# Splitting the tokens beside the norm, sorting them in one run, and another order of the expert slots

## The chip, the core and the metric

One core of a Trainium2 chip runs the whole kernel in one launch. The metric is the device time in microseconds of that launch. All data are 32-bit floats in HBM; 32 experts of 12 MiB each lie there, of which only those that some token chose are read.

## The reference

A decoder layer on 256 tokens of 2048 features. Its first half mixes a dilated attention (1024 columns) with a gated linear recurrence (1024 columns), projects the two and normalises:

```python
x = _layer_norm(ALPHA * x + mix, ln1_g, ln1_b)
moe = _hier_moe(x.reshape(B * S, D), router_grp_w, ..., w1, w3, w2)
x = _layer_norm(ALPHA * x + moe, ln2_g, ln2_b)
```

`_hier_moe` takes the best of 4 groups for each token, then the best 2 of that group's 8 experts, and adds up the two experts' outputs with their weights. One expert is

```python
(jax.nn.silu(xblk @ w1[e]) * (xblk @ w3[e])) @ w2[e]      # w1, w3: 2048 x 512, w2: 512 x 2048
```

So 512 (token, expert) pairs are spread over up to 32 experts, unevenly: on these inputs 28 experts have tokens.

## The kernel before, in words

The first half of the layer (input projection, recurrence, attention, output projection, L73 to L473) ends at about 402 us and is not touched. What follows is:

**Norm (L476 to L487).** The statistics give `rstd` and `nmr`. ScalarE normalises `X` (128 partitions, 2 token tiles, 2048 columns) in place, in four instructions: 512 and then 1536 columns for each tile.

**Router (L488 to L611).** On DVE and TensorE, with small tiles: the logits, the best group, the best two experts, each pair's place in the order by expert (`place`), and the one-hot matrices `srt` (128 x 512, one for each token tile), which put every token into its two places. `ints` holds the counts and the slots' experts; L592 writes the count of experts in use, which every engine loads at L1013 before the slots begin. L597 and L603 are two small exponentials on ScalarE for the weights. The gains' and the residual's rows come over GpSimd's queue (L642, L644). Up to L641 or so the order on each engine is a planner's, by readiness; from `manual_schedule` in `experts` on it is that of the code.

**Slots (L1014 to L1035).** The experts run one after the other in 32 slots: experts 0 and 1 first, then by rank in size, in the order of `_R` (L37): slot 2 + k takes the expert of rank `_R[k]`, rank 0 being the largest. The order mixes large with small. A slot's code has arms by its count of tokens: 32 rows (`up32`, matmuls at L824), 64 rows (`up64`, L846), 128 (`up128`, L868) and twice 128. Slots 0, 1 and those of rank 0 to 6 choose among arms by the count; rank 7 to 14 always take 64 rows, and rank 15 on 32. With 28 experts in use, ranks 0 and 1 take 128 rows, ranks 2 to 14 take 64, the other 13 slots 32. A slot's matmuls of w1 and w3 come in four quarters, with two weight tiles each; then a transpose, the silu, the matmuls of w2 (L911), and the sums into `X` through matmuls with the one-hot `ohT` (L921, L926).

**Ring (L697 to L750).** The weights come in loads of 1 MiB, 12 for an expert, on SyncE's queue, in order, into a ring of 15 tiles. `advance` (L751) says how many tiles TensorE has given back; a load whose tile is free is issued, else the queue waits. After 15 loads a sixteenth tile (`spare`, slot18, which holds the split tokens and `srt` until slot 0 is over) joins in.

**Sort (L759 to L775), called by slot 0.** For each of 16 groups of 128 columns: ScalarE copies the group into `hi` in a rounded form (L766), DVE takes the rest `lo` (L767), four matmuls with `srt` (L770) put the tokens in order, DVE or ScalarE evicts with gain and offset (L773, L775). `hi` and `lo` have two buffers in `parts`. In slot 0, `before(q)` calls `sort` ahead of each quarter of the expert's own matmuls, and the tables of `by_slot` (L614, matmuls at L195 and L628) and the residual (L799, matmuls at L808) between them; each of the four arms has this code.

Of the kernel before, what the change touches and what calls it, by code (L numbers as in the profile page):

```python
# [9 lines left out]
FT = mybir.dt.float32  # L10
# [10 lines left out]
D = 2048  # L21
# [15 lines left out]
_R = [15, 0, 16, 1, 17, 2, 3, 18, 4, 5, 19, 6, 7, 20, 8, 9, 21, 10, 11, 22, 12, 13, 14] + list(range(23, 30))  # L37
# [42 lines left out]
def hybrid_layer(ctx, tc, x, w_in, conv_w, conv_b, lru_wa, lru_ba, lru_wx, lru_bx, lru_lambda,  # L80
# [403 lines left out]
    for c in (slice(0, 512), slice(512, D)):  # L484
        for t in range(2):
            a = X[:, t, c]
            nc.scalar.activation(a, a, AF.Identity, bias=nmr[:, t:t + 1], scale=rstd[:, t:t + 1])  # L487
    ar = slot(19, "ar19")  # L488
# [57 lines left out]
    parts = slot(18, "parts", FR)  # L546
# [101 lines left out]
    experts(ctx, tc, X, acc, ar, blk, parts, srt, by_slot, Rs, Gs, ints, gb, lnr, w1, w3, w2, ident, iota, slot, sm, misc, bank,  # L648
# [31 lines left out]
def experts(ctx, tc, x1, acc, f, blk, parts, srt, by_slot, Rs, Gs, ints, gb, lnr, w1, w3, w2, ident, iota, slot, sm, misc, bank,  # L680
# [4 lines left out]

    xs = [slot(i, f"xs{i}").rearrange("p (j s) -> p j s", j=4) for i in (8, 11, 9, 12)]

    xt = slot(6, "xt").rearrange("p (j c) -> p j c", j=16)
    hl = parts[:, 0:1024].rearrange("p (b h t m) -> p b h t m", b=2, h=2, t=2)
# [7 lines left out]
        "xp": Rot(bank[0:2]),  # L697
# [10 lines left out]
    xv = x1.rearrange("p t (q m j) -> p t q j m", q=4, j=4)  # L708
# [41 lines left out]
    def advance(n=0):  # L750

        done[0] += n
        while nxt[0] < len(order) and need[nxt[0]] <= done[0]:
            load(nxt[0])
            nxt[0] += 1
# [4 lines left out]
    def sort(q):  # L760

        for jj in range(4):
            j = 4 * q + jj
            hi, lo = (hl[:, j % 2, h] for h in range(2))
            src = xv[:, :, q, jj, :]
            nc.scalar.activation(hi, src, AF.Copy)  # L766
            nc.vector.tensor_tensor(out=lo, in0=src, in1=hi.bitcast(FT), op=OP.subtract)  # L767
            xp = R["xp"].tile()
            for k, (t, part) in enumerate(((0, hi), (1, hi), (0, lo), (1, lo))):
                nc.tensor.matmul(xp, lhsT=part[:, t, :], rhs=srt[t], start=k == 0, stop=k == 3)  # L770
            dst = xs[q][:, jj, :]
            if jj % 2:
# [184 lines left out]
    side = [None]  # L957

    def expert(i):

        def before(q):
            if i == 0:
                for k in ((0, 1), (2,), (3,), ())[q]:
                    sort(k)
                    fetch(0, 0, quarters=(k,))
                if q in (1, 2):
                    next(side[0])
                if q == 3:
                    residual(0, 1)

        def small(up, n):
            if i == 0:
                side[0] = by_slot()
            else:
                ahead(i + 1)
            gt, ohT = up(i, before)
            if i == 0:
                ahead(1)
                residual(2, 3)
            dn(i, gt, ohT, n)  # L980

        def first():
            if i == 0:
                list(by_slot())
                for q in range(4):
                    sort(q)
                residual(0, 1, 2, 3)

        def wide():
            first()  # L990
            gt, ohT = up128(i, 0, True)
            ahead(i + 1)
            dn(i, gt, ohT, 128)

        def huge():
            first()
            done[0] += 8
            halves = [up128(i, c, False) for c in (0, 128)]
            ahead(i + 1)
            for c, (gt, ohT) in enumerate(halves):  # L1000
                dn(i, gt, ohT, 128, c == 1)
        arms = [(32, lambda: small(up32, 32)), (64, lambda: small(up64, 64)), (128, wide), (256, huge)]
        if i < 2:
            choose(count(81 + i), arms)
        elif bound(i) > 64:
            choose(count(32 + i), arms[1:])
        else:
            evs.clear()
            arms[bound(i) > 32][1]()
            evs.clear()  # L1010

    advance()
    n_all = nc.values_load(ints[0:1, 80:81], min_val=2, max_val=32, skip_runtime_bounds_check_because=WHY)  # L1013
    for i in range(TAIL):  # L1014
        if i < 2:
            expert(i)
            if not i:
                spare = slot(18, "ring18")
                homes[:] = [spare if t is None else t for t in homes]
            continue  # L1020
# [54 lines left out]
```

## Time and profile before

| | us |
|---|---|
| median of 3 runs | 1373.0 (1368.92 to 1380.15) |
| the profiled execution | 1368.74 |
| its span, first to last instruction | 1366.9 |
| TensorE busy | 1192.3 (87%) |
| DVE, ScalarE, GpSimd busy | 493.9, 308.3, 71.0 |
| bytes moved by DMA | 419.80 MB |

Busy shares are averages over stages with different limits: the first half of the layer (to 402 us) has TensorE as its limit, and the slots have to be read by themselves, by what the weights' queue and TensorE wait for.

### The profile page before, as it was taken

What the parts mean: (1) busy time and instruction counts of PE and PEld (TensorE: products, weight loads), DVE (VectorE), ACT (ScalarE), POOL (GpSimd) and SP (SyncE); (2) the same over time, 40 slices, a digit from 0 to 9 for tenths busy, and PEclk for the clock granted to TensorE, in tenths of its full rate; (3) what the DMA queues carried; (4) which work ended last, traced back from release to release, by engine and by line L of the source; (5) the groups of instructions that cost most, each with busy time, mean ns of one, the idle gap of its engine ahead of it and who ended that gap; (6) DMA issues with size and microseconds to landing.
All of it is one profiled execution on the core that took longest, in us unless ns stands there. A gap on an engine that the chain in (4) does not pass through costs nothing. (4 is left out here: it accounts for less than half of the span.)

```text
span 1366.9 us, 16357 instructions
## 1 busy us (share of the span) xinstructions
PE 1192.3 (87%) x6065; PEld 645.8 (47%) x6065; DVE 493.9 (36%) x776; ACT 308.3 (23%) x554; POOL 71.0 (5%) x75
## 2 busy tenths in 40 slices
PE   6989999999985777999987897788899897998875
PEld 6988899988872332333432222222333332332222
DVE  4678545457544342121121111121322212213336
ACT  4366444434332211011110100110201101100001
POOL 5111102130000000000000000000000000000001
PEclk9999999999995778999999989999999898999775
DMA  9634653464840469979889999899999999999992
GB/s 317 197 138 140 203 182 131 130 247 155 316 146 1 149 231 420 417 306 421 306 344 402 371 421 365 334 421 401 418 420 420 418 420 420 419 420 420 419 382 96
DMA packets 81721, 419.80 MB, mean 307 GB/s; under 512 B 7008, under 2 KB 7344, under 8 KB 38448
## 3 DMA queue, kind: packets, MB, share of 16 engines
q1 hardware_dynamic: 80384, 416.31, 77.0%
q0 software_dynamic: 912, 1.31, 0.5%
q8 instruction: 70, 1.15, 0.3%
q10 hardware_dynamic: 288, 0.48, 0.1%
q14 instruction: 67, 0.55, 0.1%
HBM read 432.75 MB, written 2.10 MB: 318 GB/s over the span
## 5 line engine op out<-in xcount | busy, mean ns | idle before, releaser
L926 DVE TENSOR_TENSOR xres<-bank,xres 128x512 f32<-128x512 f32 x224 | 145.7, 685 | 243.8 <-PE bank L921 243.2
L846 PE MATMUL bank<-ring,xt 128*64 128x512 f32 x792 | 203.4, 655 | 16.6 <-issue 16.6
L921 PE MATMUL bank<-sm,ar 32*128 32x512 f32 (+2 forms) x448 | 174.6, 742 | 20.0 <-DVE xres L926 10.0
L911 PE MATMUL bank<-ring,sm 128*32 128x512 f32 (+2 forms) x840 | 163.6, 625 | 32.0 <-DVE sm L858 12.1
L165 DVE TENSOR_TENSOR wl<-raw,wh 128x2048 fp32r<-128x2048 f32 (+1 forms) x59 | 129.6, 2202 | 106.3 <-ACT wh L164 106.3
L195 PE MATMUL bank<-xh,wl 128*128 128x256 f32 x512 | 148.2, 291 | 6.2 <-DVE wl L165 6.2
L195 PE MATMUL bank<-xh,wh 128*128 128x256 f32 x512 | 148.9, 291 | 1.2 <-ACT wh L164 1.2
L195 PE MATMUL bank<-xl,wh 128*128 128x256 f32 x512 | 148.4, 290 | 0.0
L824 PE MATMUL bank<-ring,xt 128*32 128x512 f32 x768 | 115.3, 690 | 31.2 <-issue 25.7
L164 ACT ACTIVATE wh<-raw 128x2048 fp32r<-128x2048 f32 (+1 forms) x59 | 107.6, 1826 | 146.7 <-PE bank L195 128.5
L846 PEld LDWEIGHTS bank<-ring,xt 128*64 128x64 f32 x792 | 64.5, 151 | 146.9 <-issue 146.8
L899 DVE COPY ar<-bank 128x256 f32<-128x256 f32 x28 | 11.9, 424 | 317.6 <-PE bank L898 317.6
L921 PEld LDWEIGHTS bank<-sm,ar 32*128 32x128 f32 (+2 forms) x448 | 64.4, 209 | 123.4 <-DVE xres L926 69.7
L911 PEld LDWEIGHTS bank<-ring,sm 128*32 128x32 f32 (+2 forms) x840 | 48.3, 130 | 124.5 <-issue 76.6
L195 PEld LDWEIGHTS bank<-xh,wl 128*128 128x128 f32 x512 | 101.0, 198 | 7.1 <-DVE wl L165 6.8
L195 PEld LDWEIGHTS bank<-xh,wh 128*128 128x128 f32 x512 | 101.3, 198 | 1.8 <-ACT wh L164 1.6
L195 PEld LDWEIGHTS bank<-xl,wh 128*128 128x128 f32 x512 | 101.3, 198 | 0.4
L824 PEld LDWEIGHTS bank<-ring,xt 128*32 128x32 f32 x768 | 28.8, 123 | 102.8 <-issue 95.3
L917 ACT ACTIVATE sm<-bank 128x512 f32<-128x512 f32 x47 | 28.1, 597 | 201.8 <-PE bank L911 193.8
L851 ACT ACTIVATE sm<-bank 128x512 f32<-128x512 f32 x13 | 7.8, 597 | 273.7 <-PE bank L846 273.7
L868 PE MATMUL bank<-ring,xt 128*128 128x512 f32 x120 | 57.8, 641 | 0.0
L674 POOL TENSOR_TENSOR xres<-xres,offset 128x512 f32<-128x512 f32 x4 | 6.4, 1611 | 940.5 <-ACT xres L673 940.5
(274 smaller groups left out, 1170.3 us busy)
## 6 DMA issues: line engine op xcount, KB each, us to landing
ring<-in_w_dram SPq DMA_DIRECT2D x330, 1024.0 KB
raw<-in_w_in_dram SPq DMA_DIRECT2D x39, 1024.0 KB
misc<-in_w_dram SPq DMA_DIRECT2D x22, 1024.0 KB
raw<-in_w_out_dram SPq DMA_DIRECT2D x16, 1024.0 KB
xres<-in_x_dram SPq DMA_DIRECT2D x4, 512.0 KB
out_dram<-xres SPq DMA_DIRECT2D x8, 256.0 KB
raw<-in_w_in_dram SPq DMA_DIRECT2D x4, 256.0 KB
offset<-in_ln_b_dram SPq DMA_DIRECT2D x1, 1024.0 KB
```

The source lines that it names most:

```text
L164: nc.scalar.activation(h[:, e], r[:, e], AF.Copy)
L165: nc.vector.tensor_tensor(out=l[:, e], in0=r[:, e], in1=h[:, e].bitcast(FT), op=OP.subtract)
L195: nc.tensor.matmul(o, lhsT=l, rhs=r, start=start, stop=stop, skip_group_check=True)
L824: nc.tensor.matmul(hp[p0:p0 + 32, :], lhsT=xt[:, j + par, i % 2 * 64:i % 2 * 64 + 32], rhs=wp(i, nm, j + par), start=j == 0, stop=j == 14)
L846: nc.tensor.matmul(hp[c * 64:c * 64 + 64, :], lhsT=xt[:, j, i % 2 * 64:i % 2 * 64 + 64], rhs=wp(i, nm, j), start=j == 0, stop=j == 15)
L851: nc.scalar.activation(hs, hp, AF.Copy)
L868: nc.tensor.matmul(hp[k], lhsT=xt[:, j, :], rhs=wp(i, nm, j), start=j == 0, stop=j == 15)
L899: nc.vector.tensor_copy(ohT, tr[:, 0:2, :])
L911: nc.tensor.matmul(yp[n * h:n * h + n, :], lhsT=gt[:, j, 0:n], rhs=w[:, c:c + 512], start=j == 0, stop=j == 3)
L917: nc.scalar.activation(y, yp, AF.Copy)
L921: nc.tensor.matmul(cp, lhsT=ohT[n * h:n * h + n, t, :], rhs=y[n * h:n * h + n, :], start=True, stop=True)
L926: nc.vector.tensor_tensor(out=a, in0=cp, in1=a, op=OP.add)
```

## The change

The normalisation goes by quarters of 512 columns, and behind each quarter its two blocks of 256 columns (4 blocks of 128 x 2 tiles wide) are split: ScalarE copies `hi`, GpSimd subtracts `lo`, one instruction for each token tile. Seven blocks of 1024 have room (`parts`, and slots 9, 12 and 6, which get their old use after the sort); the eighth is split into the first one's place when that is sorted. The sort runs in one piece ahead of slot 0 for every arm, on four PSUM banks, with the two steps of `by_slot` after blocks 2 and 4. Then come the gather for slots 0 and 1, the sixteenth ring tile, and the slots. `early` loads the two counts of slots 0 and 1 ahead of that of the experts.

```diff
-_R = [15, 0, 16, 1, 17, 2, 3, 18, 4, 5, 19, 6, 7, 20, 8, 9, 21, 10, 11, 22, 12, 13, 14] + list(range(23, 30))
+_R = [15, 16, 17, 0, 18, 19, 1, 20, 2, 3, 4, 21, 5, 6, 7, 8, 22, 9, 10, 11, 12, 13, 14] + list(range(23, 30))
...
-    for c in (slice(0, 512), slice(512, D)):
+    parts = slot(18, "parts", FR)
+    stage = [parts[:, 0:1024]]
+    for i in (9, 12, 6):
+        b = slot(i, f"stage{i}", FR)
+        stage += [b[:, 0:1024], b[:, 1024:2048]]
+    stage.append(stage[0])
+    xv = X.rearrange("p t (q m j) -> p t q j m", q=4, j=4)
+
+    def split(b):
+        hi, lo = (stage[b][:, 512 * h:512 * h + 512].rearrange("p (t j m) -> p t j m", t=2, j=2) for h in range(2))
+        src = xv[:, :, b // 2, b % 2 * 2:b % 2 * 2 + 2, :]
         for t in range(2):
-            a = X[:, t, c]
+            nc.scalar.activation(hi[:, t], src[:, t], AF.Copy)
+        for t in range(2):
+            nc.gpsimd.tensor_tensor(out=lo[:, t], in0=src[:, t], in1=hi[:, t].bitcast(FT), op=OP.subtract)
+        return hi, lo
+    jobs = []
+    for q in range(4):
+        for t in range(2):
+            a = X[:, t, q * 512:q * 512 + 512]
             nc.scalar.activation(a, a, AF.Identity, bias=nmr[:, t:t + 1], scale=rstd[:, t:t + 1])
+        for b in (2 * q, 2 * q + 1):
+            if b < 7:
+                jobs.append(split(b))
...
-        "xp": Rot(bank[0:2]),
+        "xp": Rot(bank[0:4]),
...
-    homes = list(ring)
+    homes = ring + [None]
     need = [0] * len(homes)
     for k in range(len(order)):
         homes.append(homes[k])
         need.append(k + 1)
-        if k == 13:
-
-            homes.append(None)
-            need.append(k + 2)
...
-    def sort(q):
-
-        for jj in range(4):
-            j = 4 * q + jj
-            hi, lo = (hl[:, j % 2, h] for h in range(2))
-            src = xv[:, :, q, jj, :]
-            nc.scalar.activation(hi, src, AF.Copy)
-            nc.vector.tensor_tensor(out=lo, in0=src, in1=hi.bitcast(FT), op=OP.subtract)
-            xp = R["xp"].tile()
+    def sort(b):
+
+        q = b // 2
+        hi, lo = jobs[b]
+        xps = [R["xp"].tile() for _ in range(2)]
+        for jj, xp in enumerate(xps):
             for k, (t, part) in enumerate(((0, hi), (1, hi), (0, lo), (1, lo))):
-                nc.tensor.matmul(xp, lhsT=part[:, t, :], rhs=srt[t], start=k == 0, stop=k == 3)
+                nc.tensor.matmul(xp, lhsT=part[:, t, jj, :], rhs=srt[t], start=k == 0, stop=k == 3)
+        if b == 0:
+            jobs.append(split(7))
...
         def before(q):
-            if i == 0:
-                for k in ((0, 1), (2,), (3,), ())[q]:
-                    sort(k)
-                    fetch(0, 0, quarters=(k,))
-                if q in (1, 2):
-                    next(side[0])
-                if q == 3:
-                    residual(0, 1)
+            if i == 0 and q == 3:
+                residual(0, 1)
...
     advance()
+    early = [count(81 + i) for i in range(2)]
     n_all = nc.values_load(ints[0:1, 80:81], min_val=2, max_val=32, skip_runtime_bounds_check_because=WHY)
+    xs = []
+    side = by_slot()
+    for b in range(8):
+        sort(b)
+        if b in (2, 4):
+            next(side)
+
+    xt = slot(6, "xt").rearrange("p (j c) -> p j c", j=16)
+    fetch(0, 0)
+    ahead(1)
+    spare = slot(18, "ring18")
+    homes[:] = [spare if t is None else t for t in homes]
+    advance()
```

## Rows read from the trace of the kernel before

**Rows 1.** Windows: stretch, length, busy PE PEld DVE ACT POOL, PEclk, DMA share, GB/s.

```profile
404.00:440.00 36.00, 17.50 (x57) 10.88 (x58) 16.71 (x75) 12.83 (x19) 1.63 (x3) 0.59 0.09 30
440.00:520.00 80.00, 61.98 (x332) 27.77 (x335) 28.23 (x51) 15.02 (x33) 0.00 (x0) 0.78 0.53 202
520.00:950.00 430.00, 368.12 (x1498) 134.98 (x1492) 86.32 (x156) 47.94 (x138) 0.00 (x0) 0.90 0.93 378
950.00:1330.00 380.00, 340.93 (x1608) 113.52 (x1608) 99.82 (x182) 43.55 (x129) 0.00 (x0) 0.91 1.01 419
```

**Rows 2.** Timeline of SyncE's queue: start us, us, the weights' loads issued.

```profile
403.47 0.33 SPq L748 DMA_DIRECT2D misc<-in_w_dram  x1
444.47 47.49 SPq L748 DMA_DIRECT2D ring<-in_w_dram  x9
...
1314.93 0.33 SPq L746 DMA_DIRECT2D ring<-in_w_dram  x1
```

**Rows 3.** Waits of SyncE's queue, 404 to 450: us, times, longest us.

```profile
SPq L748 <- PE bank L824: 28.0, 1, 28.0
```

**Rows 4.** Timeline of ScalarE: the norm, and the sort's first copy.

```profile
404.23 4.63 ACT L487 ACTIVATE xres<-xres,st 128x512 f32<-128x512 f32 x4 [0.36 <-DVE st L482]
...
416.60 0.65 ACT L766 ACTIVATE parts<-xres 128x256 fp32r<-128x256 f32 x1 [7.54 <-DVE ar L591]
```

**Rows 5.** Groups of instructions by line and shape, 416 to 475.

```profile
L770 PE MATMUL bank<-parts 128*128 128x512 f32 x64 | 25.9, 533 | 19.6 <-ACT parts L766 16.6 <-DVE parts L767 3.0
L766 ACT ACTIVATE parts<-xres 128x256 fp32r<-128x256 f32 x16 | 9.9, 646 | 7.5 <-DVE ar L591 7.5
...
L195 PE MATMUL bank<-ar,sm 32*128 32x32 f32 x8 | 1.9, 399 | 1.5 <-DVE sm L630 1.5
...
L628 PE MATMUL bank<-con,ar 128*32 128x128 f32 x4 | 1.0, 414 | 0.0
```

**Rows 6.** Timeline of TensorE: matmul spacing, slot 0's end, first matmuls of slots.

```profile
391.95 0.40 PE L195 MATMUL bank<-wh,al 128*128 128x512 f32 x1
392.18 0.39 PE L195 MATMUL bank<-wl,ah 128*128 128x512 f32 x1
...
474.65 3.37 PE L808 MATMUL bank<-ones,con 48*128 48x128 f32 x24
...
480.10 3.05 PE L824 MATMUL bank<-ring,xt 128*32 128x512 f32 x16
...
506.93 3.28 PE L824 MATMUL bank<-ring,xt 128*32 128x512 f32 x16 [4.87 <-issue]
...
555.41 2.08 PE L868 MATMUL bank<-ring,xt 128*128 128x512 f32 x2
...
610.64 1.93 PE L824 MATMUL bank<-ring,xt 128*32 128x512 f32 x16 [1.62 <-issue]
...
631.10 2.93 PE L868 MATMUL bank<-ring,xt 128*128 128x512 f32 x3
...
743.75 16.37 PE L846 MATMUL bank<-ring,xt 128*64 128x512 f32 x64 [5.67 <-issue]
...
780.27 3.64 PE L824 MATMUL bank<-ring,xt 128*32 128x512 f32 x16 [5.18 <-issue]
...
805.38 3.68 PE L846 MATMUL bank<-ring,xt 128*64 128x512 f32 x7
```

**Rows 7.** Timeline of GpSimd and DVE: GpSimd's two-input form, the gains' load.

```profile
30.34 3.21 DVE L165 TENSOR_TENSOR wl<-raw,wh 128x2048 fp32r<-128x2048 f32 x1 [1.20 <-ACT wh L164]
31.38 3.05 POOL L354 TENSOR_TENSOR sm<-sm,misc 128x384 f32<-128x384 f32 x1
...
38.51 0.81 POOL L644 DMA_DIRECT2D gb<-in_ln_g_dram  x1
...
291.81 1.00 POOL L354 TENSOR_TENSOR sm<-sm,misc 128x384 f32<-128x384 f32 x1
```

**Rows 8.** Timeline of TensorE's weight loads: the last wait for a load.

```profile
1335.49 0.16 PEld L911 LDWEIGHTS bank<-ring,sm 128*32 128x32 f32 x8 [2.32 <-DMA ring<-in_w_dram]
```

More of the change, by code (lines that the diff above doesn't have):

```diff
@@ L544, in hybrid_layer @@
     nc.vector.tensor_reduce(out=place, in_=pk, op=OP.add, axis=AX.X)
-    parts = slot(18, "parts", FR)
     srt = [parts[:, 1024 + 512 * t:1536 + 512 * t] for t in range(2)]
@@ L647, in hybrid_layer @@
     acc = [X[:, t, :] for t in range(2)]
-    experts(ctx, tc, X, acc, ar, blk, parts, srt, by_slot, Rs, Gs, ints, gb, lnr, w1, w3, w2, ident, iota, slot, sm, misc, bank,
+    experts(ctx, tc, X, acc, ar, blk, jobs, split, srt, by_slot, Rs, Gs, ints, gb, lnr, w1, w3, w2, ident, iota, slot, sm, misc, bank,
             con[:, C_TWO:C_TWO + 64], bst)
@@ L677, in hybrid_layer, with experts @@
         nc.sync.dma_start(ov[:, t, n * 512:n * 512 + 512], a)
-def experts(ctx, tc, x1, acc, f, blk, parts, srt, by_slot, Rs, Gs, ints, gb, lnr, w1, w3, w2, ident, iota, slot, sm, misc, bank,
+def experts(ctx, tc, x1, acc, f, blk, jobs, split, srt, by_slot, Rs, Gs, ints, gb, lnr, w1, w3, w2, ident, iota, slot, sm, misc, bank,
             two, bst):
@@ L684, in experts @@
     ring = [slot(i, f"ring{i}") for i in (0, 1, 2, 3, 7, 10, 16, 17, 13, 15, 20, 14, 4, 5)] + [misc]
-    xs = [slot(i, f"xs{i}").rearrange("p (j s) -> p j s", j=4) for i in (8, 11, 9, 12)]
-    xt = slot(6, "xt").rearrange("p (j c) -> p j c", j=16)
-    hl = parts[:, 0:1024].rearrange("p (b h t m) -> p b h t m", b=2, h=2, t=2)
     R = {
@@ L707, in experts @@
     wv2 = w2.rearrange("l e (j p) n -> p (l e) j n", p=128)
-    xv = x1.rearrange("p t (q m j) -> p t q j m", q=4, j=4)
     pieces = {}
@@ L752, in advance @@
         done[0] += n
-        while nxt[0] < len(order) and need[nxt[0]] <= done[0]:
+        while nxt[0] < len(order) and need[nxt[0]] <= done[0] and homes[nxt[0]] is not None:
             load(nxt[0])
@@ L758, in wp @@
         return pieces[i, nm, j // 4][:, j % 4 * 512:j % 4 * 512 + 512]
-    def sort(q):
-        for jj in range(4):
-            j = 4 * q + jj
-            hi, lo = (hl[:, j % 2, h] for h in range(2))
-            src = xv[:, :, q, jj, :]
-            nc.scalar.activation(hi, src, AF.Copy)
-            nc.vector.tensor_tensor(out=lo, in0=src, in1=hi.bitcast(FT), op=OP.subtract)
-            xp = R["xp"].tile()
-            for k, (t, part) in enumerate(((0, hi), (1, hi), (0, lo), (1, lo))):
-                nc.tensor.matmul(xp, lhsT=part[:, t, :], rhs=srt[t], start=k == 0, stop=k == 3)
-            dst = xs[q][:, jj, :]
-            if jj % 2:
+    def sort(b):
[3 more added lines that the diff above has]
+        for jj, xp in enumerate(xps):
+            for k, (t, part) in enumerate(((0, hi), (1, hi), (0, lo), (1, lo))):
+                nc.tensor.matmul(xp, lhsT=part[:, t, jj, :], rhs=srt[t], start=k == 0, stop=k == 3)
+        if b == 0:
+            jobs.append(split(7))
+        if b % 2 == 0:
+            xs.append(slot((8, 11, 9, 12)[q], f"xs{q}").rearrange("p (j s) -> p j s", j=4))
+        for jj, xp in enumerate(xps):
+            j = 2 * b + jj
+            dst = xs[q][:, j % 4, :]
+            if jj:
                 nc.vector.tensor_scalar(dst, xp, gb[:, 0, j:j + 1], gb[:, 1, j:j + 1], op0=OP.mult, op1=OP.add)
@@ L955, in choose @@
         evs.clear()
-    side = [None]
     def expert(i):
         def before(q):
-            if i == 0:
-                for k in ((0, 1), (2,), (3,), ())[q]:
-                    sort(k)
-                    fetch(0, 0, quarters=(k,))
-                if q in (1, 2):
-                    next(side[0])
-                if q == 3:
-                    residual(0, 1)
+            if i == 0 and q == 3:
+                residual(0, 1)
         def small(up, n):
-            if i == 0:
-                side[0] = by_slot()
-            else:
+            if i:
                 ahead(i + 1)
@@ L977, in small @@
             if i == 0:
-                ahead(1)
                 residual(2, 3)
@@ L983, in first @@
             if i == 0:
-                list(by_slot())
-                for q in range(4):
-                    sort(q)
                 residual(0, 1, 2, 3)
@@ L1003, in expert @@
         if i < 2:
-            choose(count(81 + i), arms)
+            choose(early[i], arms)
         elif bound(i) > 64:
@@ L1016, in experts @@
             expert(i)
-            if not i:
-                spare = slot(18, "ring18")
-                homes[:] = [spare if t is None else t for t in homes]
             continue
```

## The prediction

> **What bounds the kernel now.** I read the view of stretches first, then the DMA queue's issues and waits, then TensorE's slot starts. From 950 to 1330 us the core loads at 419 GB/s with a DMA share of 1.01 [rows 1]: this is the ceiling, and one load of 1 MiB costs 1.0486 MB / 419 GB/s = 2.50 us there. 28 slots run, so 28 x 12 = 336 loads, 15 of them (the ring's first fill) issued by 403.47 [rows 2]. The other 321 need 321 x 2.50 = 803.5 us. They start at 444.47, because the queue waits 28.0 us for the first two tiles that slot 0's matmuls (L824) give back [rows 2, 3]. The last load is issued at 1314.93 and TensorE waits for it until 1335.49 [rows 2, 8]. So the stage ends with the loads, and every microsecond in which the queue had nothing to issue is on the path. There are three such places:
> - 404 to 440: 30 GB/s, nothing to issue.
> - 440 to 520: 202 GB/s, so 80 x (1 - 202/419) = 41.4 us lost. Slot 0 gives its tiles back in drips, since a quarter of the sort stands ahead of each quarter of its matmuls.
> - 520 to 950: 378 GB/s, 430 x (1 - 378/419) = 42.1 us lost. Here the ring is full and TensorE is slower than the loads.
>
> Check: 440 + 41.4 + 42.1 + 803.5 = 1327, against 1335.49, of which the last load's own flight (20.6 us from issue to wait's end, not 2.5) explains the rest.
>
> **The split and the sort.** In the old form 16 groups each go ScalarE copy (0.65), DVE subtract, four matmuls, one eviction, through two small buffers: the 64 matmuls wait 19.6 us, 16.6 of it for ScalarE, at a granted clock of 0.59 over 404 to 440 [rows 1, 5]. With slot 0's own matmuls between them this begins at 416.60 and is over shortly before 474.65 [rows 4, 6]. The new form splits seven of eight blocks before the sort. ScalarE: eight normalisations at 4.63/8 = 0.58 and 14 copies at 0.65 = 13.7 us, from 404.23 to 418; before it idled 7.54 us up to 416.60 [rows 4, 5]. So ScalarE is nearly hidden behind the router, which runs on DVE until some 416. GpSimd: 14 subtracts of 256 elements. No row shows a strided one. The nearest, 128x384 from two contiguous tiles, takes 1.00 us; the longest of that form 3.05 [rows 7]. By size 0.67; I take 0.8, so 11.2 us, done at about 418; ends 0.67 and 3.05 (9.4 and 43 us). A sort's block is needed only every 2 us, so up to some 1.5 us each stays hidden. The five small DMAs of GpSimd's queue that stand behind these in the code serve the gains (issued at 38.51, so the planner puts them ahead of all this [rows 7]) and the residual's rows, first used behind slot 0's third quarter: hidden. The subtracts leave DVE, where only matmuls waited for them (3.0 us) [rows 5].
>
> What the subtracts can hurt is the router, on DVE at the same time. The row of 3.05 us ran beside a DVE subtract with two SBUF inputs, which took 3.21 itself; alone the same GpSimd form takes 1.00 [rows 7]. So the two engines hold each other up, and the router's end, for which ScalarE waits before the sort, is late by something between 0 and all 11.2 us. I take a third, 3.7: most router instructions read 32 or 64 elements, or PSUM. The Trainium skill (SBUF — State Buffer, "Who interferes with whom") says that the pair of ports is an exclusive lock and the later of the two blocks until the first is done; the trace's 3.05 beside 1.00 agrees. By it alone each two-input router step could wait for a whole subtract, the sum would take the 11.2, and the end would come 7.5 us later than I say.
>
> So the sort starts at 416.6 + 3.7 = 420.3. Its 64 matmuls of 128x512 stand 0.23 us apart at full clock (391.95 to 392.18) [rows 6]. The granted clock is 0.59 over 404 to 440, with little work there, and 0.78 behind it [rows 1], so a start at the lower of the two levels (1.2 instead of 2.4 GHz) is likely. I take 7 matmuls at twice 0.23 (3.2 us) and 57 at 0.23 (13.1), an estimate. The slot tables inside the sort add 1.0 + 1.9 of matmuls and and, as an estimate, 1.5 for the copy between them [rows 5], in all 20.7: end at 441. Bounds: all at full clock 14.7 + 4.4, all at the low one 29.4 + 4.4, so 439.4 to 454. Evictions (8 on each of two engines, four banks) stay beside it. A sixteenth buffer joins the ring there at 441, where it came 14 loads later before. Gathering the tokens and the branch, 3 us: slot 0 starts at 444 with nothing of the sort left.
>
> Slot 0 now: three quarters of 16 matmuls (3.28 at 506.93; I take 3.4 and twice half of it, 6.8), the residual's pair (474.65 to 480.10, 5.45): 456.3. Then, as before, 26.8 from the last quarter at 480.10 to the next slot's start at 506.93 [rows 6]: slot 1 at 483, 24 us earlier. Loads by then: one at 441, six from 447.5 to 451, two at 458, four from 467: 13 x 2.5 = 32.5 us between 441 and slot 1's first release at 485, about 11 lost. The queue is then as far as if it had started at 441 + 11 = 452 and never stopped; before, at 440 + 41.4 = 481.4. **Worth: 29.4 us.**
>
> **The order of the slots.** A slot needs 30 us of loads. TensorE spends 20.5 on a slot of the 32-row arm (610.64 to 631.10), 55.2 on one of 128 rows (555.41 to 610.64), 36.5 on one that chooses its 64-row arm (743.75 to 780.27, with 5.18 for leaving it) and 25.1 on a small one behind that (780.27 to 805.38) [rows 6]. The fixed 64-row slots lie at 950 to 1330, where nothing is lost. The ring's lead over TensorE, in us of loads, changes by -9.5, +25.2, +6.5 and -4.9. The ring holds 40, but nothing comes back for some 10 us at each slot's end, so I let it count as full at 30 and book the rest as lost. Old order, from a full ring at slot 1: 26.6, 17.1, wide over by 12.3, 20.5, wide over by 15.7, 20.5, two over by 3.5, 25.1, two over by 1.6 and 6.5, 25.1, one over by 1.6: 41.2 in all, against 42.1 read. New order: 26.6, 17.1, 7.6, 0, wide 25.2, two small 6.2, wide over by 1.4, 20.5, three over by 3.5 and 6.5, 25.1, two over by 1.6 and 6.5: 19.5. **Worth: 21.7 us.**
>
> That books no wait on TensorE where the lead is 0 and 6.2; there loads come late by part of their 20.6 us in flight, and what TensorE loses overflows behind the next wide slot. Bounds 0 and 16; I take 8 (the middle: no row shows such a wait before the last slots).
>
> **Sum.** 29.4 + 21.7 - 8 = 43 us, against the profiled execution of 1368.7 (span 1366.9 and 1.8 around it). The stage after the last load is unchanged. The median shown is 4.3 above it: 1373 - 43 = **1330 us**.
>
> **Rivals.** (1) A hindered start: the sort stays at the low clock (+13) and the router waits for all of the subtracts (+7.5): 1350. For it: 0.59 at 404 to 440; against: there the sort had gaps, now it has few. (2) The gain is handed back: starved small slots keep TensorE waiting at four places (slots 3, 4, 7 and 8) by 8 to 11 us each and the three chosen 64-row slots in a row meet a full ring anyway; with that some 38 of 43 are gone, 1368. For it: the lead is used up twice; against: while TensorE waits the queue is busy, so only overflow counts. (3) Nothing waits: no lock, no late load: 1330 - 3.7 - 8 = 1318. (4) Slower: GpSimd's strided subtract. The source steps by four elements, which no GpSimd row does, and all 16 subtracts gate the sort's end. It decides from (441 + 43 - 406)/16 = 4.9 us each, counted from the first copy at 406; at 6.5 the sort ends at 510, 69 later: 1330 + 69 = 1399. For it: a form never seen, and 3.05 once; against: ScalarE's strided copy costs 0.65, no multiple of its others.
> The Trainium skill (GPSIMD Engine Reference, "Performance pitfalls for Q7 kernels") puts a step of over 8 bytes at about half more per element. No run so far shows it. By it a subtract would be an estimated 1.0 us, far below what decides.
>
> **Chances.** Forecast 0.60 (1315 to 1345 on its own); (1) 0.15, (2) 0.08, (3) 0.12, (4) 0.05. Of (2) about 0.01 lies under 1359. A change of 1% is about what a measurement of this kernel can tell. Faster by over 1%: 0.60 + 0.15 + 0.12 + 0.01 = 0.88; within 1%: 0.07; slower: 0.05. The range runs from below (3) to above (1): 1307 to 1354.
>
> **What would show it.** Right: 14 subtracts under about 1.5 us beside the router; 64 sort matmuls without slot matmuls between them, ending at 438 to 445; slot 1 starting near 483; over 350 GB/s from 445 to 520; over 395 GB/s in the 430 us behind; 419 to the last load. Wrong: a sort that waits for GpSimd, the router's end past 425, TensorE waits on loads of many us in slots 3 to 8, or a queue that waits as long behind the three 64-row slots as it did behind the wide ones.

## The result, and the profile after

| | before | after | forecast |
|---|---|---|---|
| median, us | 1370.96 (4 runs, 1368.60 to 1380.15) | 1336.10 (4 runs, 1327.08 to 1341.23) | 1330 |
| the profiled execution, its span | 1368.74, 1366.9 | 1341.23, 1339.5 | |

The ratio is 0.9727 [0.9655, 0.9798], some 37 us off, where 43 were forecast. The profiled execution of after is the longest of its four. The two profiled executions also differ where nothing was changed: the router's sum for the counts (L542, L521 before) ran at 400.49 us in after and at 406.52 in before. So where two profiles are compared, lengths are taken between events, not from the span's start.

Windows of after, with the columns of [rows 1]:

```profile
404.00:440.00 36.00, 21.46 (x92) 16.93 (x93) 22.25 (x55) 14.52 (x25) 13.36 (x16) 0.68 0.00 1
440.00:520.00 80.00, 65.09 (x372) 28.72 (x374) 24.65 (x43) 9.74 (x28) 0.00 (x0) 0.72 0.84 335
520.00:950.00 430.00, 370.69 (x1554) 134.88 (x1548) 87.31 (x158) 48.29 (x139) 0.00 (x0) 0.89 0.95 386
950.00:1330.00 380.00, 343.11 (x1536) 117.83 (x1532) 110.00 (x202) 45.41 (x128) 2.61 (x2) 0.91 0.93 385
```

The loss against 419 GB/s in 440 to 520 fell from 41.4 us to 80 x (1 - 335/419) = 16.0. In 520 to 950 it fell only from 42.1 to 33.9. The last window is not slower loading: the loads are over before it ends. SyncE's queue and its waits up to 455 (as [rows 2, 3]), and TensorE's last wait for a load (as [rows 8]):

```profile
440.80 16.00 SPq L759 DMA_DIRECT2D ring<-in_w_dram  x9
```
```profile
SPq L759 <- PE bank L778: 22.7, 1, 22.7
```
```profile
1307.61 0.20 PEld L925 LDWEIGHTS bank<-ring,sm 128*32 128x32 f32 x8 [3.04 <-DMA ring<-in_w_dram]
```

The first new load goes out when the sort's last matmul (L778) gives back the spare tile, at 440.80, and the next eight within 16 us. The last wait for a load ends at 1307.61 instead of 1335.49.

GpSimd beside the router (as [rows 7]; L499 is the subtract):

```profile
406.88 6.05 POOL L499 TENSOR_TENSOR stage<-xres,stage 128x256 fp32r<-128x256 f32 x6
...
414.33 3.25 POOL L499 TENSOR_TENSOR stage<-xres,stage 128x256 fp32r<-128x256 f32 x4
```

A subtract takes 3.25/4 = 0.81 to 6.05/6 = 1.0 us, and 14 are done at 417.6. DVE at that time in after, and then the same steps in before (L549, L550, L587, L592 there):

```profile
400.49 0.77 DVE L542 TENSOR_TENSOR asg<-ar 128x64 f32<-128x64 f32 x1
...
405.07 3.03 DVE L569 TENSOR_SCALAR parts<-con,place 128x512 fp32r<-128x512 f32 x2
408.02 2.59 DVE L570 SCALAR_TENSOR_TENSOR parts<-con,place,parts 128x512 fp32r<-128x512 f32 x2
...
414.50 3.13 DVE L607 SCALAR_TENSOR_TENSOR ar<-ar,cs,con 32x32 f32<-32x32 f32 x1
417.56 0.13 DVE L612 CAST ints<-cs 1x1 int32<-1x1 f32 x1
```
```profile
406.52 0.23 DVE L521 TENSOR_TENSOR asg<-ar 128x64 f32<-128x64 f32 x1
...
410.56 0.88 DVE L549 TENSOR_SCALAR parts<-con,place 128x512 fp32r<-128x512 f32 x2
411.36 1.41 DVE L550 SCALAR_TENSOR_TENSOR parts<-con,place,parts 128x512 fp32r<-128x512 f32 x2
...
415.24 0.23 DVE L587 SCALAR_TENSOR_TENSOR ar<-ar,cs,con 32x32 f32<-32x32 f32 x1
415.40 0.13 DVE L592 CAST ints<-cs 1x1 int32<-1x1 f32 x1
```

From the sum to the count of experts DVE took 8.88 us before and 17.07 after. Three steps carry 6.2 of the 8.2: 3.03 for 0.88, 2.59 for 1.41, and 3.13 us for an operation on 32x32 elements that took 0.23. That last one, begun at 414.50, ends at 417.63, when all four of GpSimd's subtracts from 414.33 on are over (417.58): it was held for several of them in a row, not for one.

The sort's matmuls in 416 to 450, by shape (as [rows 5]):

```profile
L778 PE MATMUL bank<-parts,stage 128*128 128x512 f32 x48 | 14.1, 457 | 0.0
L778 PE MATMUL bank<-parts 128*128 128x512 f32 x16 | 5.7, 519 | 4.6 <-DVE ar L608 4.6
```

They never wait for the split: the one wait is for the router. Their timeline and the slots' starts (as [rows 6]):

```profile
418.11 3.75 PE L778 MATMUL bank<-parts 128*128 128x512 f32 x8 [4.59 <-DVE ar L608]
...
438.75 1.98 PE L778 MATMUL bank<-parts 128*128 128x512 f32 x8
441.82 5.36 PE L838 MATMUL bank<-ring,xt 128*32 128x512 f32 x48 [1.10 <-DVE xs L787]
...
483.51 3.64 PE L838 MATMUL bank<-ring,xt 128*32 128x512 f32 x16 [4.74 <-issue]
...
637.08 3.64 PE L838 MATMUL bank<-ring,xt 128*32 128x512 f32 x16 [4.56 <-issue]
...
742.91 1.92 PE L838 MATMUL bank<-ring,xt 128*32 128x512 f32 x16 [1.94 <-issue]
...
838.19 16.51 PE L860 MATMUL bank<-ring,xt 128*64 128x512 f32 x64 [5.82 <-issue]
...
1005.78 3.65 PE L860 MATMUL bank<-ring,xt 128*64 128x512 f32 x16
```

The sort runs from 418.11 to 440.73 without a stop, slot 0 begins at 441.82 and slot 1 at 483.51 (506.93 before). And the slots behind, one window each (2, 4, 5, 6, 7 and 8):

```profile
511.51:533.42 21.91, 19.23 (x124) 6.15 (x124) 5.18 (x9) 2.38 (x7) 0.00 (x0) 0.89 1.01 416
...
555.30:579.41 24.11, 20.41 (x124) 6.25 (x123) 6.38 (x12) 3.66 (x7) 0.00 (x0) 0.85 1.01 420
579.41:637.07 57.66, 51.69 (x119) 22.66 (x119) 9.15 (x16) 4.71 (x13) 0.00 (x0) 0.94 1.01 418
637.07:660.92 23.85, 21.17 (x122) 7.31 (x122) 5.18 (x9) 3.27 (x11) 0.00 (x0) 0.79 0.92 373
660.92:684.79 23.87, 21.25 (x124) 7.01 (x123) 6.57 (x13) 3.66 (x7) 0.00 (x0) 0.79 1.01 420
684.79:742.91 58.12, 52.64 (x120) 22.85 (x119) 9.06 (x16) 5.70 (x17) 0.00 (x0) 0.93 0.88 344
```

The second column is the slot's length: small slots take 21.9 to 24.1 us, not 20.5, and wide ones 57.7 and 58.1, not 55.2.

**One rule for the end.** At 2.50 us a load, a slot's 12 loads take 30 us. TensorE is slower than that on the sum of slots 1 to 16, and behind them the loads decide. So the end should be the start of slot 17 plus 11 x 30 and a constant, and the loss behind slot 1 should be TensorE's time for slots 1 to 16 minus 480. In before, the last full ring is at slot 14, and the same holds with slot 15 and 14 x 30. From the spans and timelines of all kernels that differ only ahead of slot 17 (the runs are told below):

| kernel | span | slot 1 | slot 17 | span - slot 17 | (slot 17 - slot 1) - 480 |
|---|---|---|---|---|---|
| after | 1339.5 | 483.5 | 1005.8 | 333.7 | 42.3 |
| r_after | 1340.1 | 485.4 | 1006.1 | 334.0 | 40.7 |
| e1_order | 1366.8 | 505.1 | 1033.4 | 333.4 | 48.3 |
| e3_dve | 1328.8 | 476.7 | 995.9 | 332.9 | 39.2 |
| e4_late | 1337.6 | 480.2 | 1004.0 | 333.6 | 43.8 |
| e7_nall | 1335.3 | 480.8 | 1002.4 | 332.9 | 41.6 |
| e8_resid | 1324.6 | 471.8 | 991.7 | 332.9 | 39.9 |
| f1_spread | 1328.8 | 479.4 | 995.3 | 333.5 | 35.9 |
| f3_layout | 1326.7 | 479.6 | 990.9 | 335.8 | 31.3 |
| g_all | 1333.9 | 484.1 | 998.0 | 335.9 | 33.9 |

In before, slot 15 starts at 972.5: the span is 394.4 behind it, and (972.5 - 506.9) - 420 = 45.6; in e2_sort (old order) 394.8 and 42.9. The fifth column holds within 3 us over spans that differ by 42. So 42.3 us of loss were left in after, against 45.6 in before: the 3.3 us between them are all that the order brought in this pair.

### The profile page after: what moved, and what is told of

Same layout as the page of the kernel before. It is cut to its first block, busy times and chain, and to the rows that moved or that the text cites. A ratio compares the mean times of both kernels' runs of the same rounds, so it can differ in the third digit from the quotient of the medians.

```text
span 1339.5 us, 16366 instructions
## 1 busy us (share of the span) xinstructions
PE 1181.3 (88%) x6065; PEld 644.3 (48%) x6065; DVE 494.2 (37%) x760; ACT 309.1 (23%) x558; POOL 89.0 (7%) x91
## 5 line engine op out<-in xcount | busy, mean ns | idle before, releaser
L860 PE MATMUL bank<-ring,xt 128*64 128x512 f32 x792 | 198.3, 640 | 22.7 <-issue 22.7
L925 PE MATMUL bank<-ring,sm 128*32 128x512 f32 (+2 forms) x840 | 169.6, 646 | 28.2 <-DVE sm L872 12.1
L935 PE MATMUL bank<-sm,ar 32*128 32x512 f32 (+2 forms) x448 | 172.6, 729 | 20.4 <-DVE xres L940 10.2
L838 PE MATMUL bank<-ring,xt 128*32 128x512 f32 x768 | 115.6, 714 | 21.9 <-issue 20.6
L860 PEld LDWEIGHTS bank<-ring,xt 128*64 128x64 f32 x792 | 63.8, 147 | 146.4 <-issue 146.4
L935 PEld LDWEIGHTS bank<-sm,ar 32*128 32x128 f32 (+2 forms) x448 | 63.9, 205 | 122.7 <-DVE xres L940 69.4
L838 PEld LDWEIGHTS bank<-ring,xt 128*32 128x32 f32 x768 | 29.2, 127 | 97.1 <-issue 95.8
L882 PE MATMUL bank<-ring,xt 128*128 128x512 f32 x120 | 58.2, 642 | 2.1 <-DMA ring<-in_w_dram 2.1
```

Source lines behind the costliest of these rows:

```text
L838: nc.tensor.matmul(hp[p0:p0 + 32, :], lhsT=xt[:, j + par, i % 2 * 64:i % 2 * 64 + 32], rhs=wp(i, nm, j + par), start=j == 0, stop=j == 14)
L860: nc.tensor.matmul(hp[c * 64:c * 64 + 64, :], lhsT=xt[:, j, i % 2 * 64:i % 2 * 64 + 64], rhs=wp(i, nm, j), start=j == 0, stop=j == 15)
L882: nc.tensor.matmul(hp[k], lhsT=xt[:, j, :], rhs=wp(i, nm, j), start=j == 0, stop=j == 15)
L925: nc.tensor.matmul(yp[n * h:n * h + n, :], lhsT=gt[:, j, 0:n], rhs=w[:, c:c + 512], start=j == 0, stop=j == 3)
L935: nc.tensor.matmul(cp, lhsT=ohT[n * h:n * h + n, t, :], rhs=y[n * h:n * h + n, :], start=True, stop=True)
```

## Experiments

All ratios are against the kernel before, timed beside it.

| run | median | ratio |
|---|---|---|
| e1_order | 1364.87 | 0.9948 [0.9922, 0.9974] |
| e2_sort | 1343.14 | 0.9784 [0.9757, 0.9811] |
| e3_dve | 1335.04 | 0.9727 [0.9701, 0.9754] |
| e4_late | 1342.27 | 0.9779 [0.9754, 0.9805] |
| r_after | 1337.96 | 0.9762 [0.9730, 0.9795] |
| e6_warm | 1450.97 | 1.0596 [1.0555, 1.0636] |
| e7_nall | 1336.32 | 0.9761 [0.9728, 0.9794] |
| e8_resid | 1335.83 | 0.9749 [0.9715, 0.9782] |
| f1_spread | 1331.50 | 0.9711 [0.9677, 0.9745] |
| f2_one_more | 1336.11 | 0.9733 [0.9695, 0.9771] |
| f3_layout | 1326.69 | 0.9663 [0.9626, 0.9700] |
| g_all | 1328.16 | 0.9696 [0.9654, 0.9739] |

**The two halves: e1_order and e2_sort.** The first is the kernel before with the new `_R` alone, the second the changed kernel with the old one.

```diff
-_R = [15, 0, 16, 1, 17, 2, 3, 18, ...
+_R = [15, 16, 17, 0, 18, 19, 1, 20, ...
```

> The kernel before with the new order of the slots alone. By the prediction's ledger the order is worth 21.7 us less 8 for late loads, so about 14 us: ratio 0.987 to 0.992, and less than 30 us lost in the 430 us from 520 to 950. Rival, read from the changed kernel, whose ring lost as much behind 520 as before (42.9 against 44.6 us by bytes): the order is worth under 5 us, ratio 0.996 or more, and the loss behind 520 stays near 40, only at other slots.

> The changed kernel with the old order of the slots: the split, the sort in one run and the early sixteenth tile alone. By the ledger 29 us of the gain stay and about 14 go: near 1342, ratio to before 0.979. Rival: all of the gain is the earlier start, and this is as fast as the changed kernel within 5 us, ratio 0.970 to 0.977.

Alone, the order is worth 0.0052 x 1370.5 = 7.1 us [3.6, 10.7], between the forecast of e1_order and its rival; the split and sort are worth 29.6 [25.9, 33.3], as forecast. Their sum, 36.7, is near the whole change (37 us by the first measurement, 33 by r_after below), so no third term between them is seen, to some 5 us. Windows of e1_order:

```profile
440.00:520.00 80.00, 62.60 (x334) 30.54 (x326) 27.36 (x50) 14.22 (x32) 0.00 (x0) 0.77 0.55 212
520.00:950.00 430.00, 370.35 (x1556) 135.11 (x1558) 86.83 (x158) 46.44 (x134) 0.00 (x0) 0.87 0.94 385
```

The first stretch is near that of before (202): without the new sort the start stays late. The second is that of after (386), 34.9 us lost where the expectation had under 30. But slot 17 starts only at 1033.4, and by the table's last column this execution lost 48.3 us behind slot 1, more than before (45.6). So the 7 us are shown by the medians alone, not by the two profiles.

That the split stands beside the norm, and that the sort runs in one piece, was never changed one without the other: how the 29.6 us divide between the two is not shown.

**The changed kernel once more: r_after.**

> The changed kernel again, beside the three below on one chip, for a narrower interval: ratio to before 0.970 to 0.980. Slot 0 took 41.7 us in the changed kernel's profile, 36.5 in the profiles of the two experiments with the same code there; if that was one execution's clock, it is near 36.5 here in about two cases of three.

With 0.9762 it lies 0.0022 below e2_sort's ratio, with the first measurement's 0.9727 0.0057. So the order on top of the sort is worth some 3 to 8 us by the medians, but the intervals overlap with e2_sort's, and it may be nothing. Slot 0 took 37.3 us: the 41.7 of after were that execution's.

**Without the lock: e3_dve.** DVE does the subtracts instead of GpSimd.

```diff
-            nc.gpsimd.tensor_tensor(out=lo[:, t], in0=src[:, t], ...
+            nc.vector.tensor_tensor(out=lo[:, t], in0=src[:, t], ...
```

> The changed kernel with the 16 subtracts on DVE instead of GpSimd. If GpSimd's subtracts hold the router up (router from the counts' matmul to the count of experts 15.8 us, before 8.6), that stretch falls back towards 9 us, unless the planner puts DVE's own subtracts (0.61 us each, 9.8 in all) into the router's way; then it is 12 to 18. Gain over the changed kernel: 7 us in the first case, none in the second. If there is no lock and the router is late for another reason, the stretch stays at 15 or more with no subtract between its steps.

DVE in this run:

```profile
407.84 2.19 DVE L499 TENSOR_TENSOR stage<-xres,stage 128x256 fp32r<-128x256 f32 x4
410.25 0.88 DVE L569 TENSOR_SCALAR parts<-con,place 128x512 fp32r<-128x512 f32 x2
```

L569 is back at 0.88, so the hold-up came from GpSimd. But a subtract takes 0.55 us of DVE itself, and the router still needs 14.44 us from sum to count, 2.6 less than after. In this execution slot 1 came 72.4 us behind the sum; in the seven profiles that have the changed kernel's router, sort and slot 0 it was 77.9 to 83.0. So the front was over 5 us shorter than in any of those, and the kernel may be faster: the ratio is that of the first measurement and 0.0035 below r_after's, with intervals that overlap. A gain of a few us is neither shown nor excluded.

**The sixteenth tile at its old place: e4_late.**

```diff
-    homes = ring + [None]
+    homes = list(ring)
...
+        if k == 13:
+            homes.append(None)
+            need.append(k + 2)
```

> The changed kernel with the sixteenth ring tile joining after 14 further loads, as before. One load fewer is issued ahead of slot 0's first release: the stretch from 440 to 520 loses about 2.5 us more, and the time rises by 0 to 3 us, which a measurement hardly tells. If the sixteenth tile were what carries the start, it would be 10 us or more.

0.9779 against 0.9762 for r_after, with intervals that overlap. Its loss in 440 to 520 (341 GB/s) was 80 x (1 - 341/419) = 14.9 us, against 16.0 in after. The spare tile's early load is worth nothing that this measurement shows.

**The front: e7_nall and e8_resid.** In the first, the count of experts is loaded behind the sort instead of ahead of it; in the second, slot 0's residual is spread over the second half of the sort.

```diff
-    n_all = nc.values_load(ints[0:1, 80:81], ...
     xs = []
...
+    n_all = nc.values_load(ints[0:1, 80:81], ...
     for i in range(TAIL):
```
```diff
         if b in (2, 4):
             next(side)
+        if b > 3:
+            residual(b - 4)
```

> The changed kernel with the count of experts loaded behind the sort instead of ahead of it, so that the sort waits for its own data alone. If the router's end (17.1 us behind the counts' matmul) holds the sort back, the sort begins some 4 us earlier against that matmul (13.5 instead of 17.6 us) and slot 0 and the time move by 2 to 4.5 us. Rival: the first evictions stand behind the router's last steps on DVE, four banks fill up, and the sort's end moves by under 1 us.

> The changed kernel with slot 0's residual (two pairs of gains and offsets) moved into the second half of the sort. The sort gets 5 to 8 us longer, slot 0 shrinks from 36.5 or 41.7 to 27 to 30, so slot 1 starts 2 to 8 us earlier, and the time follows by 2 to 8 us. Rival: DVE with 2.75 us for each residual beside the evictions becomes the sort's bound, and slot 1 starts when it did.

e7_nall: the sort began 9.0 us behind the counts' sum instead of 17.6, but slot 1 came only 2.6 us earlier than in r_after by the same measure, and the time did not change. In e8_resid, slot 1 came 71.4 us behind the sum instead of 83.0 in after and 79.5 in r_after, since slot 0's matmuls now run in one piece (64 in 7.07 us):

```profile
446.37 7.07 PE L838 MATMUL bank<-ring,xt 128*32 128x512 f32 x64
471.78 3.64 PE L838 MATMUL bank<-ring,xt 128*32 128x512 f32 x16 [5.46 <-issue]
```

Its profiled execution was the shortest of its runs, with an end 10 us earlier than r_after's by this measure, but the median is only 2 us lower. A few us of gain are not excluded; they are not shown.

**Filling TensorE: e6_warm.** One matmul of 128x128 that nothing reads stands behind each of the sums' matmuls in the 32-row arm; it adds work and leaves out none.

```diff
+                    if n == 32:
+                        nc.tensor.matmul(R["hp"]....[:, 0:128], lhsT=ident, rhs=iota[:, 0:128], ...
```

> The changed kernel with one more matmul (128x128, into a bank that nobody reads) behind each of the sums' matmuls in the 32-row arm. If small slots cost 21.9 to 24.1 us instead of 20.5, and the wide slots behind them 58 instead of 55, because the granted clock drops in the thin last third of a small slot, the filler brings small slots down to 20.5 to 21.5, the granted clock in them from 0.79 to 0.89 up to 0.93 or more, and the loss of loads from 520 to 1000 from 43 us to 30 or less: 8 to 12 us faster than the changed kernel. Rival: it is the lateness of loads that stretches them; then the filler changes no slot that is fed late, only lengthens the sums, and the time is the same or up to 10 us longer.

It was meant to show whether the small slots are long because the granted clock falls in the sums (L935), and doesn't. TensorE in slot 3 of this run:

```profile
578.24 1.12 PE L935 MATMUL bank<-sm,ar 32*128 32x512 f32 x2
579.29 0.49 PE L938 MATMUL bank<-con 128*128 128x128 f32 x2
...
582.13 2.07 PE L935 MATMUL bank<-sm,ar 32*128 32x512 f32 x2
584.13 0.80 PE L938 MATMUL bank<-con 128*128 128x128 f32 x2
584.86 2.07 PE L935 MATMUL bank<-sm,ar 32*128 32x512 f32 x2
```

Each sum and each filler leaves two rows of matmuls in the profile. One sum with its filler comes to take 2.73 us (582.13 to 584.86), and the eight sums of a small slot 17 to 20 us instead of 5.8 to 7.4. The fillers themselves slow down to the lower level, 0.80 for 0.49, though TensorE has no idle time from 575.30 on: in these back-to-back matmuls the granted clock falls all the same. The small slots took 32 to 36 us instead of 22 to 24, and the kernel became 6% slower.

**Another spread: f1_spread.** The same 16 slots ahead of slot 17, but two small ones before each wide one.

```diff
-_R = [15, 16, 17, 0, 18, 19, 1, 20, 2, ...
+_R = [15, 16, 0, 17, 18, 1, 19, 20, 2, ...
```

> The changed kernel with its small slots spread out: two of them ahead of the first wide slot and two between the wide ones (ranks 15, 16, 0, 17, 18, 1, 19, 20, 2, ...), so that the ring's lead is never used up by the ledger of the prediction, while the same 16 slots stand ahead of slot 17. Theory A (the end is TensorE's chain up to the last slot with a full ring, plus 30 us for each slot behind it; nothing in the changed kernel was starved): the chain from slot 1 to slot 17 stays at 518 to 524 us, the end at 333 to 334 us behind the start of slot 17, the time within 3 us of the changed kernel, ratio 0.972 to 0.978. Theory B (the prediction's term of 8 us for late loads in slots 3, 4, 7 and 8 is real): it goes, about 1328 us, ratio 0.968 to 0.970. Theory C (small slots in a row cost 22 to 24 us instead of 20.5 because they stand in a row): pairs would cost 21 to 22, the chain 510, ratio 0.966.

333.5 us behind slot 17, as Theory A says, but the chain is 515.9 us, not 518 to 524, and the ratio lies between those of Theories A and B. Of the five small slots 2, 3, 8, 9 and 13, none is over 22.4; 5 and 6, behind the first wide one, still take 24.2 and 24.0. So a little of Theory C holds. Of Theory B little is left: TensorE waits on no load in slots 1 to 16 here, but in r_after it did so for only 1.9 us. The gain over r_after's profile lies in TensorE's chain (4.8 us); the intervals of the two ratios overlap.

**One more small slot ahead: f2_one_more.**

```diff
-..., 5, 6, 7, 8, 22, 9, 10, ...
+..., 5, 22, 6, 7, 8, 9, 10, ...
```

> The changed kernel with the slot of rank 22 (32 rows) moved from place 18 to place 15. Theory A: eight small slots instead of seven lie in TensorE's chain before the loads take over, the start of slot 18 comes some 6 us earlier than 551 us behind slot 1, and the end follows it by 303.5 us unless the 64-row slots behind (29 to 31.5 us each against 30 of loads) fill the ring again: 3 to 7 us faster than the changed kernel, ratio 0.969 to 0.974. Rival (the order as such has no more to give, since each small slot moved ahead makes its neighbours dearer): 0, ratio 0.975 to 0.977.

0.9733 lies between the changed kernel's two ratios. Slot 18 starts 547.4 us behind slot 1, 3.7 less than in after, where 6 were expected: the moved slot took 24.5 us there (22.1 at place 18), in the place of a 64-row slot of 28.9. A gain of 3 us can't be told apart from none here.

**The layout of the arms: f3_layout.**

```diff
-            with tc.If(cv > n, preferred_fallthrough_block=False) as cmp:
+            with tc.If(cv > n, preferred_fallthrough_block=True) as cmp:
```

> The changed kernel with the arms of a choosing slot laid out in reverse in the instruction stream (the arm for most rows first, the one for fewest last, so that the short arm runs on into the next slot without a jump over the others). Theory A: TensorE's gap behind a choosing slot (5.1 to 5.9 us behind a 64-row arm, 4 to 5 behind the 32-row arms of slots 0 and 1, 1.9 to 4.6 behind a wide one) is the jump over the arms that stand behind; behind the 64-row and 32-row arms it falls to under 2, by 3.5 x 5 + 3 x 2 = 23 us, the wide ones jump over one arm as before or over more, plus 0 to 6; all of this lies in the chain up to slot 17, so the time falls by the same 15 to 23 us, ratio 0.958 to 0.965. Rival 1: the gap belongs to the entry or to the load of the count and stays, ratio 0.975 to 0.977. Rival 2: the jump now comes on entry and costs the same there, 0 to 5 slower.

TensorE's waits from 440 to 1000 us, first in after, then in f3_layout (us in total, times, longest; L838 is the 32-row arm, L860 that of 64, L882 that of 128):

```profile
PE bank L860 <- issue: 22.7, 4, 5.9
PE bank L838 <- issue: 20.8, 6, 5.3
```
```profile
PE bank L860 <- issue: 28.8, 6, 6.8
PE bank L882 <- issue: 9.3, 2, 5.1
...
PE bank L838 <- issue: 3.9, 1, 3.9
```

The gaps sum to 43.5 and 42.0 us: they don't go, as Theory A had it, but move from the exit to the entry of a choosing slot, as Rival 2 had it. Yet this has the lowest ratio of all, 0.9663, clear of r_after's, and TensorE's chain is 9.4 us shorter than in r_after, which neither rival had. The windows of slots 6 and 7 here, up to their last matmuls, say where part of that is:

```profile
634.70:656.20 21.50, 18.83 (x127) 6.88 (x128) 6.36 (x12) 3.28 (x11) 0.00 (x0) 0.87 0.91 367
656.20:680.00 23.80, 21.18 (x123) 6.98 (x122) 6.54 (x13) 3.66 (x7) 0.00 (x0) 0.79 1.01 420
```

Slot 6, now without a gap ahead of it, takes 21.5 us at 0.87, instead of 23.9 at 0.79; slot 16, behind a 64-row arm, 28.9 instead of 31.8: some 5 us together. Slot 7, behind a small slot in both, stays at 23.8. The gap had cost twice: its own length, and the matmuls behind it at the lower of the two levels. In after, 16 matmuls behind a gap of 4.56 us take 3.64, those behind one of 1.94 take 1.92: the factor is that between 1.2 and 2.4 GHz.

Slot 7 pays for the same level without a gap. Windows of after (columns as in [rows 1]), from slot 6's last sums into slot 7, and then to the end of slot 7's w2 matmuls:

```profile
655.60:665.80 10.20, 10.20 (x34) 3.43 (x38) 4.90 (x9) 0.00 (x0) 0.00 (x0) 0.50 1.01 420
665.80:677.40 11.60, 9.75 (x86) 3.19 (x78) 0.71 (x2) 1.47 (x3) 0.00 (x0) 1.00 1.01 420
```

The clock falls while slot 6 does its sums and stays low over slot 7's first matmuls: its 64 of w1 and w3 take 9.51 us, against 7.08 in the small slot of before that took 20.5. In slot 7's own sums it falls again: their last ten rows of matmuls take 5.52 us, against 4.55 there. Together that is the 3.4 us by which slot 7 is longer than that one. A small slot leaves the low level to its successor.

**Together: g_all** (e7_nall, e8_resid, f1_spread's order and f3_layout).

> The changed kernel with four edits together: the count of the experts loaded behind the sort, the residual inside the sort instead of inside slot 0, the small slots in pairs around the wide ones, and the reversed layout of the arms. Theory A (the end is the start of slot 17 plus 333.5 us, so whatever TensorE saves ahead of slot 17 comes off the time one for one): slot 1 some 8 to 12 us earlier than in the changed kernel (70 to 72 us behind the counts' sum), the chain from slot 1 to slot 17 about 511 us or less as with the reversed layout alone, the end at 333 to 334 us behind slot 17: about 15 to 20 us under the changed kernel, 1316 to 1322 us, ratio 0.959 to 0.965. Rival (what is gained at the front is given back in the first small slots, whose matmuls then wait for loads in flight): slot 1 earlier by 8 but the chain from there longer by as much, about 1327, ratio 0.966 to 0.969.

No better than f3_layout alone. The front gained little: slot 1 came 78.2 us behind the counts' sum. DVE in this run:

```profile
420.37 4.60 DVE L601 TENSOR_TENSOR cs<-cs 32x1 f32<-32x1 f32 x1
```

The sort that starts early puts its evictions (L787) into DVE's queue amid the router, and a step on 32 elements was held for 4.60 us, while GpSimd did five subtracts in a row (420.70 to 424.95), the last two of them for the eighth block, which is split behind the first sorted one. The count of experts came 20.2 us behind the sum and the sort ended 43.4 behind it, 2 later than in r_after (41.1). In this execution slot 11 took 43.0 us, against 36.9 in f3_layout; without that the chain would be shorter than f3_layout's, where it is 2.6 longer. The version to keep is f3_layout.

## Why the prediction was right, and where it was off

**The end goes with the loads: right**, and sharper than it was put. The two losses behind 440 are TensorE's excess over the loads, up to the last slot that finds the ring full; see the table of the rule.

**Split and sort: 29.4 us forecast, 29.6 measured alone.** Part of that is errors that cancel. The router's delay was taken as 3.7 us; it was 8.2, which doesn't show in the sort's start (418.1, with 420.3 said) because the router's sum came 6 us earlier in this execution. The subtracts cost 0.81 to 1.0 us (0.8 taken) and the sort waits for none of them; Rival 4's 4.9 us is far off. By the Trainium skill (GPSIMD Engine Reference, "Performance pitfalls for Q7 kernels") a strided subtract was an estimated 1.0 us; the trace is at or under that. The sort took 22.6 us where 20.7 was said; slot 0 started at 441.8 (444 said), slot 1 at 483.5 (483 said). That slot 1 hits the number is luck: counted from the router's sum it came 83.0 us behind, and 79.5 in r_after, where 483 - 406.5 = 76.5 was forecast. The loss from 440 to 520 was 16.0 us, where some 11 was said. Of Rival 1, the waiting was closer than the forecast itself: 8.2 of its 11.2. The Trainium skill (SBUF — State Buffer, "Who interferes with whom") names this exclusive lock, held for one instruction; the trace agrees on the hold, with 3.13 us beside 0.23, but it lasted through four subtracts. In e3_dve, without the hold-up, the router was still 5.6 us slower than before (14.44 for 8.88), so at the router a third of the 8.2 us was had back; what that is worth in time is not shown.

**The order: 21.7 - 8 = 13.7 us forecast, 3 to 8 measured by the medians.** Here the working fails, at a term of the sum. The ledger added slots at the prices of one row each: 20.5 for a small one, 55.2 for a wide one. By these TensorE needs 467.6 us for slots 1 to 15, 17.6 more than their loads; the 19.5 of overflow that the prediction names have 1.9 more, because the ledger stops the lead at 0. It needed 490.5 (slot 16 starts at 974.0), 22.9 more: the six small slots 2 to 4, 6, 7 and 9 are 14.5 over, the two wide ones 5.4, all others together 3.0. The old order's ledger was off by less: 41.2 for 43.9 in its slots 1 to 13. Two of the five small slots there stand behind wide ones, where the row of 20.5 (610.64 to 631.10) was read, and took 20.5 and 21.0. A second row of before, the small slot from 533.51 to 555.41 (21.9 us at a granted clock of 0.89, against 0.95), was there to be read and wasn't. The 8 us for late loads were for the most part a wrong cause: TensorE's waits on DMA in slots 2 to 9 come to 3.2 us in after and 1.9 in r_after. Such a wait can cost more than its length: slot 4 took 26.3 to 30.0 us in four runs where it waited 2.0 to 3.9 us for loads (e1_order, e3_dve, e4_late, e8_resid), and 24.0 to 24.2 in three where it waited for none (r_after, e7_nall, f2_one_more). In the sum the 8 us stood for part of the 22.9.

So Rival 2, the gain handed back, came true in good part for the order, by another way than the starving it named: small slots and wide exits became dearer. It never touched the sort's gain, which is why the sum still landed within some 6 us.

**What was to be seen.** Right: the subtracts, the sort in one piece, no wait on a split, no long wait on loads, 419 GB/s behind slot 17 (1005.8 to 1290); also the sort's end at 440.7 and slot 1's start, but these two with the help of the early sum. Wrong: 335 GB/s over 440 to 520 (343 from 445), where over 350 was named; 386 in the 430 us behind, where over 395 was. And one sign against it came: in the three 64-row slots 10 to 12 of after the queue moved 418, 396 and 340 GB/s, a loss of some 9 us, about that of the last wide slot (10.4 at 344).

**Still open:** why the granted clock falls in a small slot's sums. Waits of TensorE inside the sums need not be the reason, since in e6_warm it fell at 580 us, after 4.8 us of sums and fillers without one. Nor is it settled where all of the 9.4 us come from that f3_layout's chain is shorter.

## What to carry to other kernels

When loads and compute take turns as the limit, find the last place where the buffers are full: the end is the compute chain up to there plus the loads behind, and ahead of that place only what shortens the chain counts, while an order of the same stages matters by what it does to their own lengths. Price a stage from every row of its kind, beside the granted clock of each, not from the one nearest at hand. A gap ahead of a short stage costs its length and then the slower matmuls behind it, so put a gap that can't go where the stage behind it is limited by something else.

## What the runs showed of the hardware

**A jump costs more while the loads are dense.** Behind a choosing slot TensorE stands still with nothing that it waits for in the profile. Behind a wide slot that gap was 4.56 us with the DMA engines busy (ahead of slot 6 of after, share 1.03), and 1.94 us with the same jump and no loads in flight (ahead of slot 9, share 0.00; windows, columns as in [rows 1]):

```profile
632.52:637.08 4.56, 0.00 (x0) 0.03 (x1) 1.29 (x3) 0.00 (x0) 0.00 (x0) 0.79 1.03 417
740.97:742.91 1.94, 0.00 (x1) 0.03 (x1) 1.20 (x3) 0.00 (x0) 0.00 (x0) 1.00 0.00 0
```

In before it was 1.62 and 1.82 us behind the wide slots, also at a share of 0.00; that is part of why the wide slot 5 of after came out dearer than the row read. Behind 64-row arms, which jump over two arms instead of one, it was 5.3 to 5.9. f3_layout moved the gap with the layout of the code, so it belongs to the jump. The Trainium skill (Runtime: NRT & Kernel Launch, "Instruction fetch mechanics") says that a taken branch out of the part that is already loaded waits for a DMA fetch. The trace agrees: at each of these gaps a packet of 16 KiB moves on a queue of the kind "instruction". The DMA view of after, from 634.20 to 637.08 and from 740.00 to 740.97 (packets, MB, share of 16 engines):

```profile
q8 instruction: 1, 0.02, 2.2%
q8 instruction: 1, 0.02, 7.1%
```

The shares, of 16 DMA engines, make the packet 0.022 x 16 x 2.88 = 1.0 and 0.071 x 16 x 0.97 = 1.1 us long: it isn't slower beside the weights. It comes later. In the long gap none has begun before 634.20, 1.7 us into it; at the short one it begins ahead of the gap. What holds it back beside the weights is not shown.

**A small operation of DVE can be held for several us** beside GpSimd, until a whole row of GpSimd's subtracts is over: 3.13 us for 0.23 on 32x32 elements (four subtracts, in after), and 4.60 us for 32 elements (five, in g_all).

**Matmuls without a pause don't always keep the clock up:** in e6_warm, with a filler of 128 rows behind each sum of 32 rows, TensorE was busy from 580.1 to 593.0 us without a gap, and the granted clock there was 0.50: 2.73 us for one of each.
